# A decoder layer on one core: the loads at the start dealt to other queues, and the last column group split in two

## The chip, the cores and the metric

The kernel runs on one core of a Trainium2 chip, in one launch. The metric is the device time of the program in microseconds (us). The kernel before took 1698.23 us (median of 3 runs, 1697.18 to 1698.95). Its profiled execution took 1700.09 us, of which the span from the first to the last instruction is 1698.3 us.

The engines of a core are named as in the profile: PE is TensorE (PEld its weight loads), DVE is VectorE, ACT is ScalarE, POOL is GpSimd, SP is the engine that here issues transfers alone. A name with a q (SPq, ACTq, POOLq) is an engine's instruction queue where it issues transfers (DMA).

## What is computed

One layer of a hybrid decoder over 256 prompt tokens and 32 sample tokens (8 sequences of 4), 288 columns in all, in float32 precision:

```
proj = x @ w_in                      # D_MODEL 2048 -> 11280 columns
y_a  = (gB * conv3(gC * h)) @ w_a_out            # short convolution, with 2 rows of history
y_b  = gated_deltanet(silu(conv4(q|k|v)), ...) @ w_b_out   # 3 rows of history, state S per head
merged = sigmoid(m_a) * y_a + sigmoid(m_b) * y_b
x = layer_norm(ALPHA * x + merged @ w_o, ln1_g, ln1_b)
hid = square(relu(x @ w_up))                     # 2048 -> 8192
x = layer_norm(ALPHA * x + hid @ w_down, ln2_g, ln2_b)     # -> y_prompt, y_sample
```

The new histories and states are outputs too. The change touches how x and the histories arrive, and how the last layer norm is made.

## The kernel before

**Tiling.** Activations are held transposed: 128 features on the partitions, 16 such tiles (KT) for 2048 features, 288 columns of tokens (NT). A weight matrix is worked in groups of 256 output columns (GW). A group is cut into blocks of 4 k-tiles (KB x 128 rows x 256 columns, 512 KB). Each float32 weight is split into a high and a low part: ACT casts the block to `hi` (line 178), DVE subtracts to get `lo` (helper at line 140), and `matmuls(i)` issues three products for each k-tile and half of 128 columns: hi by x high, hi by x low, lo by x high (lines 203, 204, 205). A block is thus 8 steps of 3, 24 matmuls.

**Order.** The order is written out by hand: every engine runs its instructions in the order in which the program gives them. `blocks` lists all blocks; the loop over `i` (from line 1363) does the splits, the evacuations that are due (`at(i, f)`), then `matmuls(i)`, then the next weight load. Four buffers hold raw weights, four the high parts and four the low parts. `load(i)` is issued on SP's queue and waits until DVE has made the low part of the block that had the buffer. A list `fill` holds small jobs, and `matmuls` runs one of them after each step.

**The head.** PE turns x from rows of tokens into columns of features, in four parts `xr[0..3]` of 512 features each (`x_steps`, line 765; transposes on line 772, the high part on ACT at line 776, the low part on DVE), and the sample rows `xs4` in four pieces (`x_sample`, line 757). Part 0 is turned before the loop; parts 1 to 3 are jobs in `fill` during blocks 1, 3 and 5 (`x_fill`). The first eight blocks are interleaved so that blocks 0 and 1 need part 0, 2 and 3 part 1, 4 and 5 part 2, 6 and 7 part 3. The parts' loads stand on SP's queue between the weight loads: part 1 behind block 1's (line 737), part 2 behind block 3's (line 740), part 3 behind block 5's (line 1357). All four sample pieces are loaded from ACT's queue (lines 729 and 732). In blocks 0 to 5 the split of block i + 2 stands behind `matmuls(i)`.

The convolutions' histories and weights come by 16 loads on POOL's queue into `hwr` and `har`, each a strided piece for one quarter g of the columns, and the norm vectors by 3 more into `lnr` (lines 746 to 754). Ahead of them stands a copy of one element from `xr[2]` (line 745), so that they start when x's third part has landed. `hist_tiles` (line 792) turns them on PE ahead of block 6, lines 795, 798, 799 and, for `lnr`, 800.

**The ending.** `w_down` is worked in 4 slices of 2048 hidden features; `acc` gathers the sums over the slices together with the residual. In the last slice, `out_tiles(p)` (line 588) turns the 256 finished columns of group p back into rows of tokens, takes statistics of the prompt (line 602) and of the sample (line 618) and multiplies by the norm's gain into `Y` and `Ys`. For the sample, pieces of 128 columns from four neighbouring tiles lie as four quarters of 32 partitions; the product with the constant `quart` sums over the quarters. Group 7's evacuation and `final` (line 628) come behind the last matmul: the last 256 columns are added, turned and measured; the 16 records are aggregated (line 635); a small matrix `R` of row moments is turned (line 645) into `st5`; each of 8 output units of 128 tokens by 512 features is `Y * rs + rank1` on DVE, where `rank1` is a product of `st5` with the rows `m5` of gain and bias (line 658), and is written from SP's queue (line 696). Between the units stand the sample's steps: `moments`, `mean` (line 668), `deviation` (line 676), `scale` (lines 682 and 683) and `finish` (line 686), whose output is written by four transfers from ACT's queue (line 689).

Of the kernel before, what the change touches and what calls it, by code (L numbers as in the profile page):

```python
# [9 lines left out]
F32 = mybir.dt.float32  # L10
# [6 lines left out]
P = 128  # L17
# [23 lines left out]
def _constants():  # L41
# [31 lines left out]
    f["quart"] = (k % 32 == m % 32) * 0.25  # L73
    f["rowhi"] = np.isin(k, (0, 2, 3)) * 1.0
# [29 lines left out]
def hybrid_kernel(ctx: ExitStack, tc: tile.TileContext, A):  # L104
# [46 lines left out]
    def add_group(W, col0, row0, nk, acts, evac, width=NT):  # L151
        gi = dict(W=W, col0=col0, acts=acts, evac=evac, width=width)
        for j in range(nk // KB):
            blocks.append((gi, row0 + j * KB * P, j * KB, j == 0, j == nk // KB - 1))
# [9 lines left out]
    def load(i, step=KB):  # L164
# [4 lines left out]
        src = gi["W"][r0:r0 + KB * P, gi["col0"]:gi["col0"] + GW].rearrange("(k p) c -> p k c", p=P)  # L169
        for k in range(0, KB, step):  # L170
            sp.dma_start(t[:, k:k + step], src[:, k:k + step])
        raw[i] = t
# [14 lines left out]
    def matmuls(i):  # L187
# [7 lines left out]
        for k in range(KB):  # L195
            for t in range(2):
# [5 lines left out]
                en = last and k == KB - 1  # L202
                pe.matmul(o, wh, xh_, start=st, stop=False)  # L203
                pe.matmul(o, wh, xl_, start=False, stop=False)  # L204
                pe.matmul(o, wl, xh_, start=False, stop=en)  # L205
                if fill:
                    fill.pop(0)()
# [324 lines left out]
    def down_evac(c, p):  # L532
# [3 lines left out]
        if c == 3:  # L536
            if p == 0:
                return [f, lambda ps: None, lambda ps: out_tiles(p, ps)]
            if p == 7:
                return [lambda ps: out_tiles(p, ps)]  # L540
            hold = []

            def rest(ps):
                for g in hold:
                    for _ in g:
                        pass
                if p < 5:
                    tail_rows(p - 1)
            return [f, lambda ps: None, lambda ps: hold.extend(filter(None, [out_tiles(p, ps)])), rest]
        return [f]  # L550

    def tail_consts():
# [4 lines left out]
        gps.dma_start(ph["g2"], A["ln2_g"].to_broadcast([P, D]))  # L557
        gps.dma_start(ph["b0"], A["ln2_b"][:, 0:512].to_broadcast([P, 512]))
        gps.dma_start(ph["late"], A["cf"][:, NL:])
        for j in range(4):  # L560
            for t, n in (("gs", "ln2_g"), ("bs", "ln2_b")):
                row = A[n].rearrange("o (k j f) -> o k j f", j=4, f=P)[:, :, j, :]
                gps.dma_start(ph[t][32 * j:32 * j + 32, :].rearrange("p (k f) -> p k f", k=4),
                              row.to_broadcast([32, 4, P]))

    def tail_tiles():
        pl = ph["pool"]
        g4 = pl.tile([P, D + 256], F32R, tag="R4", name="g4")
        ph["m5"], ph["st5"] = g4[0:5, 0:D], g4[0:5, D:D + 256]
        r5 = pl.tile([P, KT * NX], F32, tag="R3", name="r5")  # L570
        ph["r5"] = r5[:, 0:2 * D].rearrange("p (a c) -> p a c", a=2)
        ph["Ys"], ph["cs"] = ph["r5"][:, 1, 0:512], ph["r5"][:, 1, 512:768]
        ph["bn"] = r5[:, 4096:4288].rearrange("p (b k s) -> p b k s", b=2, k=16)
        ph["bns"] = r5[:, 4288:4312].rearrange("p (k s) -> p k s", k=4)
        ph["sm"] = r5[:, 4320:4352]
        sp.dma_start(r5[0:3, 0:D], A["ln2_g"].to_broadcast([3, D]))
        sp.dma_start(r5[3:5, 0:D], A["ln2_b"].to_broadcast([2, D]))

    def tail_rows(n):
        c = slice(512 * n, 512 * n + 512)  # L580
        r5, m5 = ph["r5"], ph["m5"][:, c]
        raw_, lo = r5[0:5, 0, c], r5[0:5, 1, 1536:2048]
        act.copy(m5, raw_)
        tt(lo, raw_, m5, SUB)
        dve.tensor_scalar(out=m5, in0=m5, scalar1=cst("rowhi")[0:5, 0:1], scalar2=None, op0=MUL)
        stt(m5, lo, cst("rowlo")[0:5, 0:1], m5, MUL, ADD)

    def out_tiles(p, ps):
        if p == 0:
            ph["Y"] = ap_.tile([P, 2, D], F32, tag="ao", name="Y")  # L590
        Y, Ys, bn = ph["Y"], ph["Ys"], ph["bn"]
        a = ph["acc"]
        gv = [gtile()[:, 0:256].rearrange("p (b c) -> p b c", b=2) for _ in range(2)]
        if p == 7:
            for u in range(2):
                tt(a[:, 14 + u, :], a[:, 14 + u, :], ps[:, u, 0:NT], ADD)
        for u in range(2):
            for b in range(2):
                pe.transpose(gv[u][:, b, :], a[:, 2 * p + u, b * P:(b + 1) * P], ident)  # L599
        for u in range(2):  # L600
            for b in range(2):
                dve.bn_stats(out=bn[:, b, 2 * p + u, :], in_=gv[u][:, b, :])

        def scaled():
            for u in range(2):
                c = slice(256 * p + P * u, 256 * p + P * u + P)
                tt(Y[:, :, c], gv[u], bmid(ph["g2"][:, c], 2), MUL)

        w = p // 2
        if p % 2:  # L610
            cs = ph["cs"][:, (w % 2) * P:(w % 2) * P + P]
            act.copy(cs.rearrange("p (k t) -> p k t", k=4), a[:, 4 * w:4 * w + 4, NP_:NT])

        def sample():
            g2 = gtile()[:, 0:P]
            pe.transpose(g2, cs, ident)
            yield
            dve.bn_stats(out=ph["bns"][:, w, :], in_=g2)
            tt(Ys[:, w * P:(w + 1) * P], g2, ph["gs"][:, w * P:(w + 1) * P], MUL)
        if p == 7:  # L620
            ph["rest"] = scaled, sample()
            next(ph["rest"][1])
        else:
            scaled()
            if p % 2:
                return sample()

    def final():
        Y, Ys, bn, sm = ph["Y"], ph["Ys"], ph["bn"], ph["sm"]
        scaled, sample = ph["rest"]  # L630
        mv = sm[:, 0:4].rearrange("p (b s) -> p b s", b=2)
        sd, rs, r = sm[:, 4:6], sm[:, 6:8], sm[:, 8:10]
        R = ph["pool"].tile([P, 2, 5], F32R, tag="mv", name="R")
        for b in range(2):
            dve.bn_aggr(out=mv[:, b, :], in_=bn[:, b])
        act.activation(sd, mv[:, :, 1], AF.Sqrt, bias=epsc[:, 0:1])
        act.copy(R[:, :, 3:5], bc(ones[:, 0:2], 2))
        scaled()
        dve.reciprocal(out=rs, in_=sd)
        stt(r, mv[:, :, 0], -1.0, rs, MUL, MUL)  # L640
        stt(R[:, :, 0:2], bc(mv[:, :, 0], 2), -1.0, bc(rs, 2), MUL, MUL)
        tt(R[:, :, 2], r, R[:, :, 0], SUB)
        pr = gtile()
        for b in range(2):
            pe.transpose(pr[0:5, b * P:(b + 1) * P], R[:, b, :].bitcast(F32), ident)
        act.copy(ph["st5"], pr[0:5, 0:256])
# [3 lines left out]
        stt(t0, ph["g2"][:, 0:512], r[:, 0:1], ph["b0"], MUL, ADD)  # L650
        units = [(b, n) for b in range(2) for n in range(4)]
        rank1 = {0: t0}

        def prepare(i):
            if i < 8:
                b, n = units[i]
                rank1[i] = gtile()
                pe.matmul(rank1[i], ph["st5"][:, b * P:(b + 1) * P], ph["m5"][:, 512 * n:512 * n + 512],
                          start=True, stop=True)


        def moments():
            next(sample, None)
            dve.bn_aggr(out=mq, in_=ph["bns"])

        def mean():
            pq = gtile()
            pe.matmul(pq[:, 0:2], cst("quart"), mq, start=True, stop=True)
            act.copy(me, pq[:, 0:2])

        def deviation():
            tt(dv, mq[:, 0:1], me[:, 0:1], SUB)
            tt(dv, dv, dv, MUL)
            tt(vb, me[:, 1:2], epsc[:, 0:1], ADD)
            pq = gtile()
            pe.matmul(pq[:, 0:1], cst("quart"), dv, start=True, stop=True)
            act.activation(ds, pq[:, 0:1], AF.Sqrt, bias=vb)

        def scale():
            dve.reciprocal(out=qs, in_=ds)  # L680
            stt(ts, me[:, 0:1], -1.0, qs, MUL, MUL)
            act.mul(ph["gs"], ph["gs"], ts)
            gps.tensor_tensor(out=ph["gs"], in0=ph["gs"], in1=ph["bs"], op=ADD)

        def finish():
            stt(Ys, Ys, qs, ph["gs"], MUL, ADD)
            ys = A["y_sample"].rearrange("b t (k j f) -> (b t) k j f", j=4, f=P)
            for j in range(4):
                act.dma_start(ys[:, :, j, :], Ys[32 * j:32 * j + 32, :].rearrange("p (k f) -> p k f", k=4))

        steps = {0: moments, 1: mean, 2: deviation, 4: scale, 7: finish}
        prepare(1)
        for i, (b, n) in enumerate(units):
# [772 lines left out]
```

## Time and profile before

| | before |
|---|---|
| median of 3 runs | 1698.23 us |
| profiled execution | 1700.09 us |
| its span | 1698.3 us |
| mean granted PE clock | 0.994 |
| busy: PE, DVE, ACT, POOL | 99%, 60%, 43%, 8% |
| moved by DMA | 279.69 MB, mean 165 GB/s |

In a row of the timeline the columns are start and duration in us, the engine, the line of the kernel, the operation, and output <- inputs by tile name; in square brackets is the idle time of that engine just before, and what ended it. In a table of groups, `x8 | 4.7, 587 | 7.9` reads: 8 instructions, 4.7 us busy, 587 ns each, 7.9 us of idle time ahead of them. PEclk is the clock that PE was granted, 1.00 being full. A row of transfers gives the queue, how many, the size of one, and the us from issue to landing; q0 is POOL's queue of transfers, q1 SP's, q10 ACT's.

### The profile page before, as it was taken

How to read it: one execution, taken by the hardware profiler on the slowest of the kernel's cores; microseconds unless marked ns; L12 is line 12 of the kernel's file. 1: busy time of each engine (PE TensorE's matmuls, PEld its weight loads, DVE VectorE, ACT ScalarE, POOL GpSimd, SP SyncE). 2: the span in 40 equal slices, each digit the busy share in tenths (PEclk: the TensorE clock that was granted, in tenths of full speed). 3: DMA queues.
4: the chain of work that ended last, by engine and by line, in shares of the span. 5: the costliest groups of instructions: out<-in, count | busy, mean ns of one | idle time of the engine just before them, and what ended most of it. 6: DMA issues, size and time to landing. Idle time of an engine off the chain costs nothing.

```text
span 1698.3 us, 31025 instructions
## 1 busy us (share of the span) xinstructions
PE 1681.4 (99%) x13036; PEld 1665.4 (98%) x13036; DVE 1011.8 (60%) x1295; ACT 726.7 (43%) x1048; POOL 132.6 (8%) x223
## 2 busy tenths in 40 slices
PE   8999999999999999999999999999999999999997
PEld 7999999999999999999999999999999999999996
DVE  4687886757544444556778744565445554466565
ACT  4785526344533333334445533344334433344331
POOL 2231422113300000000010000000000000000000
PEclk9999999999999999999999999999999999999998
DMA  9464476535655555555575555555555555555552
GB/s 268 126 199 138 114 203 199 148 106 165 194 164 163 170 164 163 168 161 163 169 194 177 168 163 166 169 162 163 169 166 161 166 169 164 163 166 159 172 158 72
DMA packets 272997, 279.69 MB, mean 165 GB/s; under 512 B 12185, under 2 KB 268121, under 8 KB 272725
## 3 DMA queue, kind: packets, MB, share of 16 engines
q1 hardware_dynamic: 267082, 265.26, 52.4%
q0 software_dynamic: 4352, 11.67, 2.5%
q8 instruction: 102, 1.67, 0.4%
q10 hardware_dynamic: 1424, 0.79, 0.2%
q14 instruction: 37, 0.30, 0.0%
HBM read 270.19 MB, written 7.48 MB: 164 GB/s over the span
## 4 chain that ended last, share of the span: by engine, by line
PE 97%; DMA 2%; DVE 0%; issue 0%; SPq 0%; POOL 0%; ACTq 0%; ACT 0%
PE acc L203 31%; PE acc L205 31%; PE acc L204 31%; DMA xr<-in_x_prompt_dram 1%; PE g L1078 1%; DMA hwr<-in_state_gdn_conv_dram 1%; PE g L1066 0%; PE g L1225 0%; PE g L1245 0%; PE g L1248 0%; DMA lnr<-in_gdn_norm_w_dram 0%; PE g L820 0%; PE g L1197 0%; PE g L1237 0%; PE g L599 0%; PE g L947 0%
## 5 line engine op out<-in xcount | busy, mean ns | idle before, releaser
L140 DVE TENSOR_TENSOR lo<-raw,hi 128x1024 fp32r<-128x1024 f32 (+1 forms) x500 | 614.5, 1232 | 550.6 <-ACT hi L178 548.4
L178 ACT CAST hi<-raw 128x1024 fp32r<-128x1024 f32 (+1 forms) x496 | 517.2, 1045 | 760.6 <-PE acc L204 704.9
L203 PE MATMUL acc<-xh,hi 128*128 128x288 f32 x1408 | 421.9, 300 | 0.0
L204 PE MATMUL acc<-xl,hi 128*128 128x288 f32 x1408 | 416.5, 296 | 1.0 <-DVE xl L140 1.0
L205 PE MATMUL acc<-xh,lo 128*128 128x288 f32 x1408 | 416.8, 296 | 0.0
L203 PE MATMUL acc<-dh,hi 128*128 128x290 f32 x1024 | 303.9, 297 | 0.0
L204 PE MATMUL acc<-dl,hi 128*128 128x290 f32 x1024 | 303.2, 296 | 0.0
L205 PE MATMUL acc<-dh,lo 128*128 128x290 f32 x1024 | 302.7, 296 | 0.0
L205 PE MATMUL acc<-hh,lo 128*128 128x288 f32 x1024 | 302.3, 295 | 0.0
L204 PE MATMUL acc<-hl,hi 128*128 128x288 f32 x1024 | 302.3, 295 | 0.0
L203 PE MATMUL acc<-hh,hi 128*128 128x288 f32 x1024 | 302.2, 295 | 0.0
L204 PEld LDWEIGHTS acc<-xl,hi 128*128 128x128 f32 x1408 | 265.8, 189 | 2.1 <-DVE xl L140 1.2
L203 PEld LDWEIGHTS acc<-xh,hi 128*128 128x128 f32 x1408 | 265.6, 189 | 2.0 <-issue 0.7
L205 PEld LDWEIGHTS acc<-xh,lo 128*128 128x128 f32 x1408 | 265.5, 189 | 0.2 <-DVE lo L140 0.2
L203 PEld LDWEIGHTS acc<-dh,hi 128*128 128x128 f32 x1024 | 193.6, 189 | 0.1
L205 PEld LDWEIGHTS acc<-dh,lo 128*128 128x128 f32 x1024 | 193.3, 189 | 0.0
L204 PEld LDWEIGHTS acc<-dl,hi 128*128 128x128 f32 x1024 | 193.3, 189 | 0.1
L204 PEld LDWEIGHTS acc<-hl,hi 128*128 128x128 f32 x1024 | 192.5, 188 | 0.0
L205 PEld LDWEIGHTS acc<-hh,lo 128*128 128x128 f32 x1024 | 192.3, 188 | 0.0
L203 PEld LDWEIGHTS acc<-hh,hi 128*128 128x128 f32 x1024 | 192.1, 188 | 0.0
L204 PE MATMUL acc<-ml,hi 128*128 128x288 f32 x256 | 75.6, 295 | 0.0
L205 PE MATMUL acc<-mh,lo 128*128 128x288 f32 x256 | 75.6, 295 | 0.0
(395 smaller groups left out, 1606.9 us busy)
## 6 DMA issues: line engine op xcount, KB each, us to landing
raw<-in_w_in_dram SPq DMA_DIRECT2D x175, 512.0 KB, 3.8
raw<-in_w_up_dram SPq DMA_DIRECT2D x128, 512.0 KB, 3.8
raw<-in_w_down_dram SPq DMA_DIRECT2D x128, 512.0 KB, 3.7
raw<-in_w_o_dram SPq DMA_DIRECT2D x32, 512.0 KB, 4.0
raw<-in_w_a_out_dram SPq DMA_DIRECT2D x16, 512.0 KB, 3.7
raw<-in_w_b_out_dram SPq DMA_DIRECT2D x16, 512.0 KB, 3.6
S<-in_state_gdn_dram POOLq DMA_DIRECT2D x8, 512.0 KB, 6.6
out_dram<-S POOLq DMA_DIRECT2D x8, 512.0 KB, 4.6
```

The costliest lines, as they stand in the source:

```text
L140: dve.tensor_tensor(out=out, in0=a, in1=b, op=op)
L178: act.copy(his[i][:, k:k + step], raw[i][:, k:k + step])
L203: pe.matmul(o, wh, xh_, start=st, stop=False)
L204: pe.matmul(o, wh, xl_, start=False, stop=False)
L205: pe.matmul(o, wl, xh_, start=False, stop=en)
L1078: pe.matmul(out[r, q * 64:q * 64 + 64], a[r, q, :], b[r, q, :], start=True, stop=True)
```

## The change

In the head, parts 1 to 3 of x are loaded from POOL's queue, each behind a copy of one element of the part before it, so that they run in turn; three of the sample pieces follow part 1 there, and the histories follow part 3. The histories come by 4 loads of contiguous rows, with the order of rows in `hwr` and `har` changed and the copies out of PSUM rearranged to it. SP's queue holds weight loads in one row. The splits of two blocks stand together behind blocks 1, 3 and 5, behind x's copies, the even block in quarters; one empty job in `fill` is gone.

```diff
-    for c in range(1, 4):
-        act.dma_start(xs4[:, c * P:c * P + P], xsr[c])
...
-    load(1)
-    sp.dma_start(xr[1], xpr[:, :, 512:1024])
-    load(2)
-    load(3)
-    sp.dma_start(xr[2], xpr[:, :, 1024:1536])
+    for i in range(1, 4):
+        load(i)
...
-    gps.tensor_copy(hwr[0:1, 0:1], xr[2][0:1, 0, 0:1])
-    for g in range(4):
-        c, c2 = slice(768 * g, 768 * g + 768), slice(256 * g, 256 * g + 256)
-        gps.dma_start(hwr[28 * g:28 * g + 24, :], A["state_gdn_conv"][0].rearrange("b j c -> (b j) c")[:, c])
-        gps.dma_start(hwr[28 * g + 24:28 * g + 28, :], A["gdn_conv_w"][0][:, c])
-        gps.dma_start(har[19 * g:19 * g + 16, :], A["state_conv_a"][0].rearrange("b j c -> (b j) c")[:, c2])
-        gps.dma_start(har[19 * g + 16:19 * g + 19, :], A["conv_a_w"][0][:, c2])
+    for i in range(1, 4):
+        gps.tensor_copy(xr[i][0:1, 0, 0:1], xr[i - 1][0:1, 0, 0:1])
+        gps.dma_start(xr[i], xpr[:, :, 512 * i:512 * i + 512])
+        if i == 1:
+            for c in range(1, 4):
+                gps.dma_start(xs4[:, c * P:c * P + P], xsr[c])
+    gps.tensor_copy(hwr[0:1, 0:1], xr[3][0:1, 0, 0:1])
+    gps.dma_start(hwr[0:96, :], A["state_gdn_conv"][0].rearrange("b j (g c) -> (b j g) c", g=4))
+    gps.dma_start(hwr[96:112, :], A["gdn_conv_w"][0].rearrange("j (g c) -> (j g) c", g=4))
+    gps.dma_start(har[0:64, :], A["state_conv_a"][0].rearrange("b j (g c) -> (b j g) c", g=4))
+    gps.dma_start(har[64:76, :], A["conv_a_w"][0].rearrange("j (g c) -> (j g) c", g=4))
...
-    sp.dma_start(xr[3], xpr[:, :, 1536:2048])
...
-            fill.extend([idle, idle, a_, s_, idle, b_])
+            fill.extend([idle, a_, s_, idle, b_])
...
         matmuls(i)
+        if i in (1, 3, 5):
+            for u, step in ((i + 1, 1), (i + 2, KB)):
+                split_hi(u, step)
+                split_lo(u, step)
         if i < 6:
-            split_hi(i + 2)
-            split_lo(i + 2)
             load(i + 6)
```

In the ending, the last group of 256 columns becomes two groups of 128, each of 2 blocks of 8 k-tiles (the same 24 matmuls for a block). The first of them is evacuated and turned beside the last group's matmuls; its 15 records of statistics are put together early, so that `final` joins one result with one new record. Tiles 0 to 7 are no longer multiplied by the gain as rows on DVE but as columns on ACT, and are turned again in `final`, four at a time, into a PSUM tile (`widen`) onto which the product with the row moments is added (`rank`); ACT then makes the four units of them, and DVE the other four. The sample's columns are laid out with the quarter as the fastest of the row index, so that its output is one transfer.

```diff
+    def next_to_last(ps):
+        a = ph["acc"][:, 14, :]
+        tt(a, a, ps[:, 0, 0:NT], ADD)
+
+    def collect(ps):
+        turned(14)
...
+        for b in range(2):
+            dve.bn_aggr(out=fin[:, b, 1:3], in_=bn[:, b, 0:15])
...
+    def final(ps):
+        a, fin, sm, Y, Ys, R = ph["acc"], ph["fin"], ph["sm"], ph["Y"], ph["Ys"], ph["R"]
+        for c in (slice(0, P), slice(P, NP_), slice(NP_, NT)):
+            tt(a[:, 15, c], a[:, 15, c], ps[:, 0, c], ADD)
+        scaled = turned(15, fin[:, :, 3:9])
+        sample_copy(3)
+        sample_stats, sample_scaled = sample_turn(3, 4, True)
...
+        widen(0, 0)
+        widen(0, 1)
+        widen(1, 0)
+        act.activation(sd, mv[:, :, 1], AF.Sqrt, bias=epsc[:, 0:1])
...
+        def act_unit(b, n):
             c = slice(512 * n, 512 * n + 512)
-            stt(Y[:, b, c], Y[:, b, c], rs[:, b:b + 1], rank1[i], MUL, ADD)
+            act.mul(Y[:, b, c], wide[n][:, b, :], rs[:, b:b + 1])
             sp.dma_start(A["y_prompt"][0, b * P:(b + 1) * P, c], Y[:, b, c])
...
+        dve_unit(0, 2, t0)
+        rank(wide[0][:, 0], 0, 0, 0, False)
+        act_unit(0, 0)
+        pq = gtile()
+        pe.matmul(pq[:, 0:2], cst("quart"), mq, start=True, stop=True)
+        rank(wide[0][:, 1], 0, 1, 0, False)
+        act_unit(1, 0)
+        rank(wide[1][:, 0], 0, 0, 1, False)
+        act_unit(0, 1)
+        r12 = rank_tile(1, 2)
...
+        pq2 = gtile()
+        pe.matmul(pq2[:, 0:1], cst("quart"), dv, start=True, stop=True)
+        act.activation(ds, pq2[:, 0:1], AF.Sqrt, bias=vb)
+        dve_unit(1, 2, r12)
+        widen(1, 1)
+        rank(wide[1][:, 1], 0, 1, 1, False)
+        dve.reciprocal(out=qs, in_=ds)
+        stt(ts, me[:, 0:1], -1.0, qs, MUL, MUL)
+        act.mul(Ys, Ys, qs)
+        gps.tensor_tensor(out=Ys, in0=Ys, in1=ph["bs"], op=ADD)
+        act_unit(1, 1)
...
+        dve_unit(0, 3, r03)
+        dve_unit(1, 3, r13)
+        stt(Ys, ph["gs"], ts, Ys, MUL, ADD)
+        act.dma_start(A["y_sample"].rearrange("b t (j f) -> (b t j) f", j=4), Ys)
...
+    add_group(A["w_down"][0], D - 2 * P, 3 * 2048, KT, acts_h, [next_to_last, collect], cols=P)
+    add_group(A["w_down"][0], D - P, 3 * 2048, KT, acts_h, [final], cols=P)
```

The rest of the diff gives `add_group`, `load` and `matmuls` the number of columns of a group, and sets the constants and the tiles of the ending to the new layouts.

More of the change, by code (lines that the diff above doesn't have):

```diff
@@ L161, in at, with load @@
         due.setdefault(i, []).append(f)
-    def load(i, step=KB):
+    def load(i, step=16):
         if i >= len(blocks):
@@ L201, in matmuls @@
                 st = first and k == 0
[L202 removed]
+                en = last and k == kb - 1
                 pe.matmul(o, wh, xh_, start=st, stop=False)
@@ L600, in out_tiles @@
[L600 to L630, printed above, removed]
+        a, Y = ph["acc"], ph["Y"]
@@ L651, in final @@
[L651 to L669, printed above, removed]
@@ L685, in finish @@
[L685 to L693, printed above, removed]
+        for b in range(2):
+            dve.bn_aggr(out=mv[:, b, :], in_=fin[:, b])
```

211 lines of the change are left out of this document (132 added, 79 removed).

## Prediction

> **What bounds the kernel now.** I read the page first, then the waits of TensorE (PE), then the timeline where it waits.
>
> ```profile
> span 1698.3 us, 31025 instructions
> PE 1681.4 (99%) x13036; PEld 1665.4 (98%) x13036; DVE 1011.8 (60%) x1295; ACT 726.7 (43%) x1048; POOL 132.6 (8%) x223
> L203 PE MATMUL acc<-dh,hi 128*128 128x290 f32 x1024 | 303.9, 297 | 0.0
> ```
>
> PE is busy 99% of the span, and the middle's matmul groups have 0.0 us of idle time ahead of them. Asked for the waits of PE from 43 to 1680 us, the trace gives no row at all. Neither the number of product matmuls nor their shape changes, so the middle keeps its time. What can move is the first 43 us and what follows the last matmul. In the head, PE stands still at these places (start, duration, instruction, and in brackets the wait):
>
> ```profile
> 11.76 0.29 PE L205 MATMUL acc<-xh,lo 128*128 128x288 f32 x1
> 12.59 0.63 PE L772 MATMUL g<-cf,xr 128*128 128x128 f32 x4 [0.55 <-DMA xr<-in_x_prompt_dram]
> ...
> 15.74 0.40 PE L203 MATMUL acc<-xh,hi 128*128 128x288 f32 x1
> 17.15 0.40 PE L204 MATMUL acc<-xl,hi 128*128 128x288 f32 x1 [1.01 <-DVE xl L140]
> ...
> 32.22 0.26 PE L798 MATMUL g<-cf,hwr 112*128 112x112 f32 x1
> 33.41 0.26 PE L799 MATMUL g<-cf,har 76*128 76x76 f32 x1 [0.94 <-DMA har<-in_conv_a_w_dram]
> 33.61 0.23 PE L799 MATMUL g<-cf,har 76*128 76x76 f32 x1
> 35.17 0.28 PE L800 MATMUL g<-cf,lnr 33*128 33x33 f32 x1 [1.33 <-DMA lnr<-in_gdn_norm_w_dram]
> ```
>
> Two stretches behind the last of these waits (columns: stretch, its length, PE busy and instructions, then the other engines, PEclk, DMA share, GB/s):
>
> ```profile
> 35.40:41.40 6.00, 6.00 (x26) 6.00 (x26) 0.89 (x1) 0.72 (x4) 0.84 (x2) 0.50 0.89 261
> 41.60:47.60 6.00, 6.00 (x47) 6.00 (x47) 5.07 (x9) 5.43 (x11) 1.49 (x4) 1.00 0.37 109
> ```
>
> A running matmul takes 0.13 us (47 in 6.00). From start to start, less that, the waits are 0.7 + 1.3 = 2.0 us for x's second part, and 1.1 + 1.4 = 2.5 us for the histories and norm vectors. Behind these the clock falls: at a granted clock of 0.50, 26 matmuls take 6.00 us; at 1.00 they take 26 x 6.00/47 = 3.3. That is 2.7 us more. The head thus holds **2.0 + 2.5 + 2.7 = 7.2 us**. The lateness is GpSimd's (POOL): its history loads start when x's third part has landed, then wait for earlier loads of their own queue.
>
> ```profile
> 16.88 0.18 POOL L745 COPY hwr<-xr 1x1 f32<-1x1 f32 x1 [15.97 <-DMA xr<-in_x_prompt_dram]
> 17.36 0.70 POOL L748 DMA_DIRECT2D hwr<-in_state_gdn_conv_dram  x1 [0.31 <-POOL hwr L745]
> ...
> 24.25 0.52 POOL L748 DMA_DIRECT2D hwr<-in_state_gdn_conv_dram  x1 [2.66 <-DMA hwr<-in_state_gdn_conv_dram]
> ...
> 30.17 0.49 POOL L754 DMA_DIRECT2D lnr<-in_gdn_norm_w_dram  x1
> ```
>
> **The change, head.** x's parts 1 to 3 go from SP's queue to POOL's, each behind a one-element copy that waits for the part before; behind part 1 go three 64 KB loads of the sample rows (from ACT's queue), behind part 3 the histories: 4 loads instead of 16, then 3 norm loads. What 512 KB takes on either queue:
>
> ```profile
> xr<-in_x_prompt_dram SPq DMA_DIRECT2D x1, 512.0 KB, 6.2
> ```
> ```profile
> xr<-in_x_prompt_dram SPq DMA_DIRECT2D x1, 512.0 KB, 9.1
> ```
> ```profile
> S<-in_state_gdn_dram POOLq DMA_DIRECT2D x1, 512.0 KB, 5.8
> ```
> ```profile
> S<-in_state_gdn_dram POOLq DMA_DIRECT2D x2, 512.0 KB, 7.8
> ```
> ```profile
> lnr<-in_gdn_norm_w_dram POOLq DMA_DIRECT2D x1, 0.5 KB, 4.9
> ```
> ```profile
> 4.83 0.63 PE L772 MATMUL g<-cf,xr 128*128 128x128 f32 x4
> ```
>
> The first two rows are parts 1 and 2 before; the next two are a single and two queued 512 KB loads on POOL later in this kernel (KB, then us from issue to landing). I take 5.8 us a part, since only one is in flight, and keep 7.8 and SP's worst for the rivals. Part 0's first half is there by 4.8 (row L772), the copy and the step to the issue take 0.5 (16.88 to 17.36), so part 1 lands at 5.3 + 5.8 = 11.1, part 2 at 17.4, part 3 at 23.7. Seven loads follow, 0.7 us for the first issue and 0.5 for each other (rows at 17.36 and 30.17): the last starts at 27.4 and, with 4.9, lands at 32.3.
>
> When PE asks: part 1's transposes come one step (three matmuls, 0.4 us) earlier in block 1 than before, at 11.5; no wait for up to 6.2 us of landing. What comes in its place is **block 1's weights**, which sit in SP's queue when POOL's part 1 starts to move. The rows: all DMA up to 7.4 us; block 1's weights before; POOL's queue (q0) from 102 to 106 us; a weight load issued at that time.
>
> ```profile
> DMA packets 1843, 1.49 MB, mean 202 GB/s; under 512 B 128, under 2 KB 1843, under 8 KB 1843
> ```
> ```profile
> 9.46 1.14 ACT L178 CAST hi<-raw 128x512 fp32r<-128x512 f32 x2 [1.10 <-DMA raw<-in_w_in_dram]
> ```
> ```profile
> q0 software_dynamic: 317, 1.17, 101.6%
> ```
> ```profile
> raw<-in_w_in_dram SPq DMA_DIRECT2D x1, 512.0 KB, 8.0
> ```
>
> At 1.17 MB in 4 us, a part's 512 KB move in 1.8 us; half of what is left of 5.8 I put ahead of the first byte, so part 1 starts near 7.4 (an estimate). 1.49 MB had moved by 7.4 us; all up to block 1's weights is 1664 KB = 1.70 MB, so 0.2 MB are left when part 1 begins. The last two rows show such a meeting: q0 moved its 1.17 MB with no SP row beside it, and the weight load took 8.0 us. So block 1's weights, which landed at 9.46 and were just in time, may wait for part 1 (1.8 us) and the sample rows (192 KB, 0.7): between 0 and 2.5 us late. I take **1.2**, halfway, as no row shows a load that is cut off near its end. The Trainium skill, "DMA: Bandwidth & Descriptors", section "Issuing engines are not separate DMA queues", has the queues interleave on the same engines and so speaks against moving a load between them; the 102 to 106 row does not show an interleaving. By the page block 1 would be some 0.7 late instead of 1.2 (an estimate: 0.2 MB at half that row's rate take 1.4 us instead of 0.7), and the time 0.5 lower.
>
> The weight splits of blocks 2 and 3, 4 and 5, 6 and 7 now come behind x's copies on ACT and DVE, in quarters for the even block.
>
> ```profile
> L776 ACT CAST xh<-g 128x512 fp32r<-128x512 f32 x8 | 4.7, 587 | 7.9 <-PE g L772 7.9
> L140 DVE TENSOR_TENSOR xl<-g,xh 128x512 fp32r<-128x512 f32 x8 | 5.5, 689 | 11.0 <-ACT xh L776 11.0
> ...
> L140 DVE TENSOR_TENSOR lo<-raw,hi 128x256 fp32r<-128x256 f32 x4 | 1.5, 420 | 0.0
> ```
>
> From the last x transposes to the first low quarter: 0.2 + 0.59 + 0.69 + 0.42 = 1.9 us. PE has three steps (1.2) and two matmuls (0.27) to do: a wait of **0.45** at blocks 2 and 4, none at 6, where history transposes stand between. Later quarters come every 0.42 us and are used every 0.8. Parts 2 and 3 are asked for at 11.5 + 1.2 + two blocks of 24 matmuls (6.4) + x's nine transposes (about 1.0) + 0.45 = 20.5 and, by the same step without the 1.2, 28.4; they are in time. PE reaches the histories at 28.4 + 2.4 + 1.0 = 31.8, the norm vectors at 32.6, against 32.3: no wait, by 0.3 us only, and no half clock. ACT's three issues fewer gain nothing (it waits for PE there). Head: 7.2 - 1.2 - 0.9 = **5.1 us less** (bounds 3.5 and 6.7).
>
> **The change, ending.** The last 256 columns become two groups of 128, so only 128 columns' worth of sums, transposes and statistics lies behind the last matmul. Before:
>
> ```profile
> 1680.71 0.82 DVE L140 TENSOR_TENSOR acc<-acc,acc 128x288 f32<-128x288 f32 x2 [5.04 <-PE acc L205]
> ...
> 1682.50 1.02 DVE L635 BATCH_NORM_AGGREGATE r<-r 128x2 f32<-128x96 f32 x2
> ...
> 1687.42 0.59 PE L668 MATMUL g<-r,g 128*128 128x2 f32 x2
> ...
> 1689.59 0.26 ACT L677 ACTIVATE r<-g,r 128x1 f32<-128x1 f32 x1 [1.39 <-PE g L676]
> ...
> 1691.08 1.27 POOL L683 TENSOR_TENSOR g<-g 128x512 f32<-128x512 f32 x1 [822.31 <-ACT g L682]
> 1692.38 0.75 DVE L143 SCALAR_TENSOR_TENSOR r<-r,g 128x512 f32<-128x512 f32 x1
> 1693.17 2.65 ACTq L689 DMA_DIRECT2D out_dram<-r  x4
> ```
> ```profile
> L143 DVE SCALAR_TENSOR_TENSOR Y<-Y,r,g 128x512 f32<-128x512 f32 x7 | 4.9, 743 | 0.1
> ```
> ```profile
> L682 ACT ACTIVATE g<-g,r 128x512 f32<-128x512 f32 x1 | 0.7, 722 | 0.4 <-DVE r L143 0.4
> ```
>
> The prompt's eight units were 0.74 us each on DVE alone; now four stay there and four go to ACT (0.72 by L682's row; before shows no such unit from PSUM). The sample's path ends last. New, counted from 1680.7: sums 0.6, transposes and statistics to 2.0, aggregates over 9 numbers instead of 96 to 2.4 (1682.50 + 1.02 stood at 2.8), square root 2.8, row moments 3.3, their transposes and copy 4.3, sample moments 4.3, first output unit on DVE to 6.3, mean product (0.59) waiting beside it to 5.7, four small steps on DVE to 6.7, second product to 7.5, square root (0.26) 7.8, DVE's unit ahead to 8.0, two small steps 8.3, ACT 0.72 to 9.1, POOL 1.27 to 10.4, DVE 0.75 to **11.2**. Before it stood at 1693.1, 12.4: 1.2 less. Its output is one transfer of 256 KB instead of four issues in 2.65 us: one is 0.66, 2.0 less; the 2.5 us from the last issue to 1698.3 stay. The prompt's last unit ends near 10.2 and its write is covered by that. Against it: two transposes more ahead of the last matmul (four in 0.63, L772), 0.3. Ending: 1.2 + 2.0 - 0.3 = **2.9 us less** (bounds 1.2 and 4.5; the unknowns are ACT's units and the order in which PE's products interlock).
>
> **Sum.** 5.1 + 2.9 = 8.0. The profiled execution took 1700.09 for its 1698.3 us of span; that run gives 1692.1. The median shown is 1.86 below it and the terms do not depend on that: 1698.2 - 8.0 = 1690.2.
>
> **Rivals.**
> - *Block 1's weights are late and the clock halves.* The clock after the first waits:
>
> ```profile
> 16.00:20.00 4.00, 2.99 (x22) 2.85 (x22) 3.33 (x6) 2.17 (x3) 2.81 (x6) 1.00 1.09 365
> ```
>
> A wait of 2.5 instead of 1.2, in a stretch like 32.2 to 35.2, and 2.7 us of half clock: 1694.2. For: the row of q0 alone. Against: the waits up to 17.15 left the clock at 1.00. The Trainium skill, "TensorE: Matmul & The Clock Gate", Part 1, asks for an idle window of some 3.4 us; here two waits of 1.1 and 1.4 with transposes between were enough, so that rule does not exclude it. 0.12.
> - *The histories are still late.* At 6.6 us a part the norm vectors land at 34.7, PE waits 2 us, the clock falls again: head 0.4, sum 3.3, 1694.9. For: the margin of 0.3. 0.08.
> - *Slower: POOL's chain is the bound.* Three parts in series cost three times the landing: the norm vectors come at 32.3 + 3 (t - 5.8). At t = 7.7 that is 38.0, where the head loses what the ending gains; at the 7.8 of queued loads it is zero, and at 9.1, SP's slowest x part, it is 42.2, 7.2 us past before: 1702.5. Against: one part in flight, and POOL's queue went first at 102. 0.05.
> - *The ending doesn't shorten but for the one output:* sample steps wait behind units on ACT and DVE, 1691.4. 0.12, and inside the forecast's range.
> - *Block 1 isn't held up (1.2 more) and the ending reaches its bound (1.6 more):* 1687.4. 0.10.
>
> **How the numbers follow.** The forecast has 0.53, 1690.2, its own range 1688.0 to 1692.3. Eight in ten: from 1687.0 to 1694.3, which leaves out the late histories, the slow chain and half of the other edges. A measurement of this kernel can tell 0.2% (3.4 us) from no change. Faster: all but the last-named late cases, 0.90; same 0.05; slower 0.05.
>
> **What would show it.** POOL's three copies at about 5, 11 and 17 us and norm loads landing by 32; no PE wait for xr, har or lnr; one for block 1's hi or lo of 0 to 2.5 us; waits of 0.4 at blocks 2 and 4; PEclk 1.00 to the end of the head; the last DMA issued some 11 us behind the last matmul. The forecast is wrong if a part takes over 6.2 us on POOL's queue, or if the last write waits for the prompt's.

## The result and the profile after

| | before | changed |
|---|---|---|
| median of 9 runs | 1698.07 us | 1693.16 us |
| lowest and highest | 1696.32 to 1699.51 | 1692.23 to 1694.74 |
| profiled execution, its span | 1700.09, 1698.3 us | 1692.23, 1690.4 us |
| mean granted PE clock of that execution | 0.994 | 0.998 |

The ratio is 0.9973 (95% interval 0.9962 to 0.9983): 4.6 us less, between 2.9 and 6.5. The forecast, 1690.2, was 8.0 less; the measured time lies in the stated range (1687.0 to 1694.3) and above the forecast's own (1688.0 to 1692.3). From profile to profile the span fell by 7.9, nearly the forecast's sum, but the profile of before is of its longest execution and that of the changed kernel of its shortest. Where the missing 3 us are is the question of the experiments.

The page of the changed kernel:

```profile
span 1690.4 us, 31072 instructions
PE 1679.0 (99%) x13054; PEld 1663.5 (98%) x13054; DVE 1008.8 (60%) x1300; ACT 734.4 (43%) x1071; POOL 128.4 (8%) x215
```

Its waits of PE in the first 43 us (in each row the total, how often, the longest; the one for `warm` is at the very start of both kernels); then POOL's queue in the same stretch:

```profile
PE g L862 <- DMA lnr<-in_gdn_norm_w_dram: 1.2, 1, 1.2
PE g L782 <- DVE warm L777: 1.2, 1, 1.2
PE g L834 <- DMA xr<-in_x_prompt_dram: 1.0, 1, 1.0
PE acc L211 <- DVE lo L140: 0.4, 2, 0.2
```
```profile
4.95 0.88 POOL L805 DMA_DIRECT2D xr<-in_x_prompt_dram  x1 [0.31 <-POOL xr L804]
...
11.73 0.17 POOL L804 COPY xr<-xr 1x1 f32<-1x1 f32 x1 [4.25 <-DMA xr<-in_x_prompt_dram]
...
18.54 0.17 POOL L804 COPY xr<-xr 1x1 f32<-1x1 f32 x1 [5.62 <-DMA xr<-in_x_prompt_dram]
...
24.13 0.35 POOL L809 COPY hwr<-xr 1x1 f32<-1x1 f32 x1 [4.38 <-DMA xr<-in_x_prompt_dram]
24.77 0.55 POOL L810 DMA_DIRECT2D hwr<-in_state_gdn_conv_dram  x1 [0.29 <-POOL hwr L809]
...
27.86 0.49 POOL L816 DMA_DIRECT2D lnr<-in_gdn_norm_w_dram  x1
```

No wait for block 1's weights, and no wait for x's parts in the loop (the 1.0 for `xr` is for part 0, ahead of the loop). The wait for the norm vectors is still there, 1.2 us, ending at 33.66. Behind it the clock is full, where the profile of before had 26 matmuls at 0.50:

```profile
35.20:41.20 6.00, 6.00 (x47) 6.00 (x46) 4.00 (x6) 3.87 (x11) 2.67 (x5) 1.00 0.89 176
```

The ending, from the last product matmul to the last issue:

```profile
1676.26 0.29 PE L211 MATMUL acc<-hh,lo 128*128 128x288 f32 x1
```
```profile
1676.59 0.58 DVE L140 TENSOR_TENSOR acc<-acc,acc 128x128 f32<-128x128 f32 x3 [0.31 <-PE acc L211]
...
1680.85 0.75 DVE L143 SCALAR_TENSOR_TENSOR Y<-Y,r 128x512 f32<-128x512 f32 x1
...
1684.45 1.41 DVE L143 SCALAR_TENSOR_TENSOR Y<-Y,r,g 128x512 f32<-128x512 f32 x2 [0.86 <-PE g L711]
1685.77 0.75 DVE L143 SCALAR_TENSOR_TENSOR r<-g,r 128x512 f32<-128x512 f32 x1
```
```profile
1681.78 1.27 ACT L715 ACTIVATE Y<-acc,r 128x512 f32<-128x512 f32 x2 [0.58 <-PE acc L711]
...
1686.55 0.36 ACTq L758 DMA_DIRECT2D out_dram<-r  x1
```

DVE takes up the last sums at 1676.59, against 1680.71 before: 4.1 us less up to there. From there to the end of the span it is 13.8 us against 17.6: 3.8 less. ACT's new units take 0.64 to 0.69 each.

### The profile page after: what moved, and what is told of

Read it like the earlier page. It is cut to its first block, busy times and chain, and to the rows that moved or that the text cites. A ratio compares the mean times of both kernels' runs of the same rounds, so it can differ in the third digit from the quotient of the medians.

```text
span 1690.4 us, 31072 instructions
## 1 busy us (share of the span) xinstructions
PE 1679.0 (99%) x13054; PEld 1663.5 (98%) x13054; DVE 1008.8 (60%) x1300; ACT 734.4 (43%) x1071; POOL 128.4 (8%) x215
## 3 DMA queue, kind: packets, MB, share of 16 engines
q8 instruction: 102, 1.67, 0.4%
## 4 chain that ended last, share of the span: by engine, by line
PE 97%; DMA 2%; POOL 0%; issue 0%; ACT 0%; DVE 0%; DVEq 0%; SPq 0%
PE acc L209 31%; PE acc L211 31%; PE acc L210 31%; DMA xr<-in_x_prompt_dram 1%; PE g L1140 1%; PE g L1128 0%; DMA lnr<-in_gdn_norm_w_dram 0%; PE g L1287 0%; PE g L1307 0%; PE g L1310 0%; PE g L882 0%; PE g L1259 0%; PE g L1299 0%; PE g L1009 0%; PE g L615 0%
## 5 line engine op out<-in xcount | busy, mean ns | idle before, releaser
L182 ACT CAST hi<-raw 128x1024 fp32r<-128x1024 f32 (+2 forms) x505 | 517.9, 1029 | 749.7 <-PE acc L210 701.0
```

The source lines that it names most:

```text
L182: act.copy(his[i][:, k:k + step], raw[i][:, k:k + step])
```

## The experiments

All times are medians. The runs come in four sets, each on one chip, and the ratio is to runs of the kernel before in the same set. Before's median was 1697.2 in the first set (the first four rows; 30 runs), 1697.6 in the second (the next four rows; 12 runs, and one of 4222.8 us that is left out), and 1697.5 in the third (the next three) and the fourth. The theory at the start (A): the terms of the sum are right, but the half clock of before's profiled execution isn't in every run. The rival (B): the head gives its 4.1 us in every run and the ending gives less than it shows.

| kernel | median (runs) | ratio, 95% interval | clocks |
|---|---|---|---|
| head alone | 1698.00 (11) | 1.0003, 0.9994 to 1.0012 | 0.993 to 0.997 |
| ending alone | 1694.43 (11) | 0.9985, 0.9976 to 0.9994 | 0.995 to 0.998 |
| norm loads first | 1692.61 (8) | 0.9973, 0.9963 to 0.9983 | 0.997, 0.998 |
| contiguous loads alone | 1693.35 (11) | 0.9979, 0.9970 to 0.9987 | 0.996, 0.997 |
| contiguous loads and ending | 1690.27 (5) | 0.9959, 0.9946 to 0.9972 | 0.997, 0.998 |
| histories behind part 2 | 1691.53 (5) | 0.9965, 0.9952 to 0.9978 | 0.998 |
| the same, old splits | 1690.15 (5) | 0.9957, 0.9944 to 0.9970 | 0.998 |
| changed kernel again | 1693.28 (9) | 0.9975, 0.9965 to 0.9985 | 0.995 to 0.998 |
| four output transfers | 1694.43 (11) | 0.9989, 0.9980 to 0.9998 | 0.995 to 0.998 |
| old splits only | 1696.29 (11) | 0.9992, 0.9984 to 1.0001 | 0.995, 0.996 |
| before again | 1698.26 (1) | | 0.995 |
| quiet head, four transfers | 1691.31 (5) | 0.9965, 0.9952 to 0.9979 | 0.997, 0.998 |

The clock is the mean over the whole span, and the ending counts in it: behind the last product matmuls the clock halves in every profile, for 13.6 to 14.9 us with the old ending and for 5.3 to 10.0 us with the new one. The stretch is shown here for contiguous loads alone (mean clock 0.996), then for the changed kernel (0.998); both have full clock in all that stands before it.

```profile
1676.80:1691.40 14.60, 5.62 (x13) 3.00 (x13) 9.15 (x24) 1.85 (x6) 1.27 (x1) 0.50 0.47 162
```
```profile
1684.50:1690.40 5.90, 0.27 (x1) 0.00 (x0) 2.02 (x3) 0.40 (x1) 1.00 (x1) 0.50 0.74 270
```

So 0.996 with the old ending, and 0.997 or 0.998 with the new one, is what profiles show whose head has no half clock; a lower mean points to half clock in the head (0.997 can be either: the profile of norm loads first has it). Clocks are to be compared between kernels of the same ending only.

**Head alone, ending alone.** The first has every edit of the first diff, with the old ending; the second every edit of the other.

> The head of the change alone, the old ending. The profiles of before and after differ by 4.1 us up to block 7. Theory A: 2.7 us of that is the half clock behind the norm vectors' wait, and only some runs of before have it, so the median falls by 1.5 to 3 us, before's runs differ in their mean clock (0.994 and 0.996), and the slower of them are those at the lower clock. Rival B: the head gives the 4.1 us in every run, and what the medians lack (4.9 instead of 7.9) is lacking in the ending: median 4.1 lower.

> The ending alone, the old head. Profiled, the time behind the last matmul fell from 17.6 to 13.9 us, with 0.3 more for two transposes ahead of it. Theory A: the median falls by 3.2 to 3.8 us. Rival B: by some 0.8 (4.9 less 4.1). My prediction had 2.9.

The head alone gains nothing, and the ending alone 2.6 us by the ratio (1.0 to 4.1). B is out: not the ending but the head lacks its gain. But A, too, had expected 1.5 to 3 from the head.

**Norm loads first.** On the changed kernel, the three norm loads go ahead of x's parts on POOL's queue:

```diff
+    gps.dma_start(lnr[0:16, :], A["ln1_g"].rearrange("o (k p) -> (o k) p", p=P))
...
     for i in range(1, 4):
         gps.tensor_copy(xr[i][0:1, 0, 0:1], xr[i - 1][0:1, 0, 0:1])
...
-    gps.dma_start(lnr[0:16, :], A["ln1_g"].rearrange("o (k p) -> (o k) p", p=P))
...
```

> The changed kernel with the three norm loads at the front of POOL's queue instead of the end. The wait of 1.2 us for the norm vectors goes; the conv weights of har are last, issued at 24.9 and landing near 30.4, PE asks at 31.6: no wait. Theory A: 1.2 to 1.5 us less than the changed kernel's 1693.2 and no run at a clock of 0.996, since the runs at 1694.5 to 1694.7 (0.996, 0.997) had a half clock behind this wait. Rival: the lower clock of those runs comes from the ending, then some runs stay 2 us above the others, and the median is 1.2 lower.

A half miss: no run has a clock under 0.997, as expected, but the median is only 0.6 lower, not 1.2 or more, and by the ratio (0.9973, as for the changed kernel) not lower at all. The wait moved to the histories:

```profile
31.82 0.57 PE L858 MATMUL g<-cf,hwr 112*128 112x112 f32 x4 [0.66 <-DMA hwr<-in_gdn_conv_w_dram]
33.43 0.26 PE L862 MATMUL g<-cf,har 76*128 76x76 f32 x1 [0.94 <-DMA har<-in_conv_a_w_dram]
```
```profile
34.10:37.40 3.30, 3.30 (x15) 3.30 (x15) 2.20 (x2) 1.61 (x5) 1.20 (x2) 0.50 0.98 207
37.60:40.60 3.00, 3.00 (x25) 3.00 (x24) 0.68 (x1) 1.66 (x4) 0.29 (x1) 1.00 0.90 220
```

So not the norm loads are late but all that stands behind part 3. The two windows show the half clock once more (PEclk 0.50, 15 matmuls in 3.30 us against 25 in 3.00), here for some 3.4 us, about half as long as in the profile of before.

**Contiguous loads alone.** On the kernel before, only the 16 history loads become the 4 contiguous ones, with the copies out of PSUM arranged to them; x stays on SP's queue:

```diff
     gps.tensor_copy(hwr[0:1, 0:1], xr[2][0:1, 0, 0:1])
-    for g in range(4):
...
+    gps.dma_start(hwr[0:96, :], A["state_gdn_conv"][0].rearrange("b j (g c) -> (b j g) c", g=4))
...
```

> The kernel before with its 16 history loads made 4 contiguous ones, nothing else. If the number of loads made the histories late: first issue at 17.4, seven issues of 0.5 to 0.7 us end at 21, all landed by 27, PE asks at 32: the 2.5 us of waits and the half clock go, the 2.0 us of waits for x stay, so the median falls by 2.5 to 4 us, about as much as by the whole head. Rival: x has to leave SP's queue for the histories to land in time; then the norm vectors still land behind 33 and the median falls by under 1 us.

The first answer holds: 3.6 us by the ratio (2.2 to 5.1), more than the whole head and nearly as much as the whole change. POOL's queue, and PE's waits, in this kernel:

```profile
15.92 0.68 POOL L746 DMA_DIRECT2D hwr<-in_state_gdn_conv_dram  x1 [0.31 <-POOL hwr L745]
...
19.13 0.48 POOL L752 DMA_DIRECT2D lnr<-in_gdn_norm_w_dram  x1
```
```profile
PE g L719 <- DVE warm L714: 1.2, 1, 1.2
PE g L770 <- DMA xr<-in_x_prompt_dram: 0.5, 1, 0.5
PE acc L204 <- DVE xl L140: 0.4, 1, 0.4
PE acc L203 <- ACT hi L1341: 0.3, 1, 0.3
```

Seven issues end at 19.6 instead of 30.7; no wait for `hwr`, `har` or `lnr` is left. The waits for x, which I had expected to stay at 2.0 us, were 0.4 in this profile (the row for `xl`; those for `xr` and `hi` are for part 0 and block 0's weights). The edit makes the loads fewer and contiguous at once; no run here tells the two apart. For the number speaks that POOL waits for landings between the 16 loads of before (2.66 us ahead of the issue at 24.25, shown in the prediction), and never between these seven. The changed kernel has the same seven loads and starts them at 24.8, because they stand behind x's part 3 on the same queue. From this I formed theory A2: of the head only the contiguous loads gain, and moving x to POOL's queue gives it back.

**Contiguous loads and ending; histories behind part 2.** The first joins the last kernel and the new ending. The second changes one line of the changed kernel, the third also takes back the moved splits and the dropped empty job:

```diff
-    gps.tensor_copy(hwr[0:1, 0:1], xr[3][0:1, 0, 0:1])
+    gps.tensor_copy(hwr[0:1, 0:1], xr[2][0:1, 0, 0:1])
```

> The 4 contiguous loads and the new ending, with x's parts on SP's queue and the splits as before. Theory A2 (of the head only the contiguous loads gain anything; moving x to POOL's queue gives it back, since the histories then start at 24.8 instead of 15.9): the two gains add, 1693.4 (contiguous alone) less 2.8 (ending alone) = 1690.6, 6.6 under before and 2 under the changed kernel, with no run below a clock of 0.998. Rival: the moves of x and the splits are worth the 2 us of waits for x in the runs that have them: 1692.5 or more, no better than the changed kernel.

> The changed kernel with the histories waiting for x's part 2 instead of 3, so that they run beside part 3. Theory A2: issues from 19.7 to 23, landing by 30; PE asks from 30.5 to 31.6: the waits for histories and norm vectors (1.9 us in the profile of the changed kernel) go, median 1690.8 to 1691.5, no run below 0.998. Rival: part 3 and the histories share POOL's queue and part 3 lands 2 us later or more, past 28.4: the wait moves to x and the median stays at 1692.5 to 1693.

> As the kernel with the histories behind part 2, with the splits and empty jobs of before. Prices the moved splits, with the histories out of the way: if the two waits for lo of 0.2 (0.39 a block) are all that they cost, 0.8 lower than that kernel; if the old order brings back waits for x's low part at blocks 2 and 4 (0.7 and 1.0 in the profiles with the old order), 0.5 to 1 higher.

The times agree with A2 and against its rivals: 1690.27, with the clock at 0.997 or 0.998 (I had expected none below 0.998); 1691.53, all five runs within 0.5 us at 0.998; and with the old splits 1690.15. The two gains add as forecast. The cause in A2 needs one correction: the last kernel has x on POOL's queue and the first on SP's, and they are equally fast. So it isn't the move of x that gives the gain back, but the place of the histories behind x's part 3. Of the splits' price neither answer was right (1.4 us, where 0.8 was the one and a gain the other): besides the waits for lo, another wait stood behind the histories with the moved splits, seen in PE's waits and ACT's timeline of the second kernel:

```profile
PE acc L209 <- ACT w L271: 1.1, 1, 1.1
```
```profile
37.33 1.05 ACT L182 CAST hi<-raw 128x1024 fp32r<-128x1024 f32 x1 [1.67 <-DMA raw<-in_w_in_dram]
```

Paired splits free the raw buffers of two blocks late and together, so the weights behind them are loaded later, and ACT waits 1.67 us for one of those. With the old splits ACT's cast ran at 34.77 and PE did not wait there.

**The changed kernel again, and before again.**

> The changed kernel once more, for a second profile and the spread of its runs beside the others on one chip. Theory A2: most runs at 1692.3 to 1693.2 with a clock of 0.998, one in three some 2 us longer at 0.996 or 0.997, each of these with one more clock window of 3.4 us at half clock behind the norm vectors. Rival: the longer runs have the clock of the others and are longer in the ending.

> The kernel before once more, for a second profile. Theory A2: the 2.0 us of waits for x and the two windows of half clock of the first profile belong to that run; most runs of before have a clock of 0.995 or 0.996 and one window or none behind the norm vectors. This one: 1695.7 to 1698, waits for x and its low part under 1.5 us, a wait for har or lnr of 2 to 3 us as before.

The median of the changed kernel came out the same, 1693.28, and its second profile is of its longest run, 1697.78, no better than before. PE in it, and the stretch behind:

```profile
34.11 0.57 PE L857 MATMUL g<-cf,hwr 112*128 112x112 f32 x4 [2.76 <-DMA hwr<-in_gdn_conv_w_dram]
35.41 0.36 PE L861 MATMUL g<-cf,har 76*128 76x76 f32 x1 [0.63 <-DMA har<-in_conv_a_w_dram]
```
```profile
35.20:41.20 6.00, 5.72 (x24) 5.43 (x25) 1.27 (x2) 0.89 (x4) 0.25 (x2) 0.50 0.89 197
```

Part 3 had landed at 25.3 instead of 24.1, the histories followed 1.9 us later than in the first profile, PE waited 3.4 us and the clock halved. Over both sets the changed kernel has 18 runs: 11 at a clock of 0.998, 1692.18 to 1693.34 us, and 7 at 0.995 to 0.997, 1693.61 to 1697.78. So the longer runs are those with the lower clock, as expected, but the longest had two stretches of 3.4 us at half clock and not one more (the row above shows all of its 6 us at 0.50), and a wait of 0.6 for x's part 1 besides.

Before's second profile, at 0.995 and 1698.26, was 0.3 above what was expected. Its waits for x are 1.0 in the loop, against 1.6 by the same view in the first profile (0.55 and 1.01); the 0.7 for `xr` is for part 0, ahead of the loop. Its half clock was shorter: 36 matmuls in the same 6 us.

```profile
PE g L800 <- DMA lnr<-in_gdn_norm_w_dram: 2.0, 1, 2.0
...
PE acc L204 <- DVE xl L140: 1.0, 1, 1.0
PE g L772 <- DMA xr<-in_x_prompt_dram: 0.7, 1, 0.7
```
```profile
35.20:41.20 6.00, 6.00 (x36) 6.00 (x35) 0.88 (x2) 1.90 (x7) 0.55 (x2) 0.72 0.88 268
```

Of before's 30 runs in the first set, 3 had the clock of the first profile, 0.994 (1698.9 to 1699.9), 15 had that of the second, 0.995, and 12 had 0.996, which with this ending is the clock of a head without half clock; among these are the seven shortest, 1695.65 to 1696.44.

**Old splits only.** The changed kernel, histories behind part 3, with the splits of before:

```diff
-        if i in (1, 3, 5):
-            for u, step in ((i + 1, 1), (i + 2, KB)):
-                split_hi(u, step)
-                split_lo(u, step)
         if i < 6:
+            split_hi(i + 2)
+            split_lo(i + 2)
             load(i + 6)
```

> The changed kernel with the splits and empty jobs of before, histories behind part 3 as changed. With the histories behind part 2 the old splits were worth 1.4 us. Theory A2: here they are worth nothing, since the histories land at 31.5 to 33.5 whatever PE did before, and what PE gains ahead of them it waits longer there: median 1692.5 to 1693.5, and as many or more runs at 0.995 to 0.997. Rival: the two gains are independent: 1691.8.

Both answers missed: it is 3 us slower than the changed kernel, with all runs at 0.995 or 0.996. The histories did not land at a time of their own. First SP's queue and the transfers from 27 to 31 us in the changed kernel, then the same two views here:

```profile
3.77 21.40 SPq L175 DMA_DIRECT2D raw<-in_w_in_dram  x6
25.22 0.50 SPq L1409 DMA_DIRECT2D cf<-in_cf_dram  x1
```
```profile
q1 hardware_dynamic: 568, 0.80, 68.5%
q0 software_dynamic: 136, 0.42, 35.7%
```
```profile
3.75 15.18 SPq L175 DMA_DIRECT2D raw<-in_w_in_dram  x6
18.98 1.73 SPq L1409 DMA_DIRECT2D cf<-in_cf_dram  x1
```
```profile
q1 hardware_dynamic: 1044, 1.37, 98.6%
q0 software_dynamic: 16, 0.10, 7.6%
```

The landing of x's part 3 and the wait of PE in this kernel:

```profile
25.85 0.51 POOL L809 COPY hwr<-xr 1x1 f32<-1x1 f32 x1 [6.21 <-DMA xr<-in_x_prompt_dram]
```
```profile
PE g L857 <- DMA hwr<-in_gdn_conv_w_dram: 3.8, 1, 3.8
```

With the old splits the raw buffers come free earlier, SP's queue is 6 us ahead (18.98 against 25.22), and what it loads runs into x's part 3 and the histories. Part 3 lands at 25.85 instead of 24.13, though it was issued at 18.9 against 19.0, so the histories are issued 1.9 us later (26.66 against 24.77); their first bytes come 3.8 us behind that instead of 2.3, and so q0 moves 0.10 MB in those 4 us instead of 0.42. PE waits 3.8 us for `hwr`. In the changed kernel SP's queue moved next to nothing from 22.4 to 25.8: the pairing of the splits, by holding it back, kept the way clear. I take this for the reason why the same edit costs 3 us there and gains 1.4 where the histories come earlier.

**Four output transfers.** On the changed kernel, then on the kernel with the histories behind part 2 and the old splits:

```diff
-        act.dma_start(A["y_sample"].rearrange("b t (j f) -> (b t j) f", j=4), Ys)
+        ys = A["y_sample"].rearrange("b t (j f) -> (b t j) f", j=4)
+        for j in range(4):
+            act.dma_start(ys[32 * j:32 * j + 32, :], Ys[32 * j:32 * j + 32, :])
```

> The changed kernel with the sample's output in four transfers of 32 rows instead of one of 128. My prediction has the one transfer at 2.0 us less (three issues of 0.66 on ACT): 1695.2 against the changed kernel's 1693.2, and the last issue starts 2 us later behind the last matmul. Rival: smaller transfers land sooner, so less than half of the 2.0 shows: under 1694.2.

> Four output transfers once more, on the kernel with the histories behind part 2 and the old splits (1690.15, all its runs at 0.998, 0.9 us between the lowest and the highest), so that the head's clock doesn't blur it. With four transfers on the changed kernel the profile had the end 0.6 us later behind the last matmul, and its medians differed by 1.2. If the four issues (1.85 us together, against 0.36 for one) delay only the last piece, which lands sooner for its size: 1690.7 to 1691.0. Rival, my prediction's term: 1692.2.

1694.43, with clocks from 0.995 to 0.998, tells little; on the quiet head (histories behind part 2, old splits) it is 1691.31 against 1690.15, 1.2 us for the one transfer (the two were measured on different chips), between the two answers. Four issues take 1.86 us, but a transfer of 64 KB landed in 1.8 us where that of 256 KB took 2.3 (1.8 to 2.1 and 2.2 to 2.8 over the profiles):

```profile
1685.09 1.86 ACTq L760 DMA_DIRECT2D out_dram<-r  x4
```
```profile
out_dram<-r ACTq DMA_DIRECT2D x4, 64.0 KB, 1.8
```
```profile
out_dram<-r ACTq DMA_DIRECT2D x1, 256.0 KB, 2.3
```

## Why the prediction was right and where it failed

The measured time lies in the range and on the forecast side, but the forecast's sum of 8.0 became 4.6 to 4.9, and the head's part of it, 5.1, is what failed: alone it gives nothing, and on top of the new ending 1.2 us by the medians (2.0 by the ratios). That the range held is in part luck. Its upper end, 1694.3, lies just above the rival of late weights of block 1 (1694.2), which did not come; the late histories, which did, I had left out of it at 1694.9.

- *The middle keeps its time*: right; no wait of PE between 43 and 1674 us.
- *"lands at 32.3 ... no wait, by 0.3 us only, and no half clock"*: this is the step that failed. The three parts took 6.8, 6.3 and 5.1 us instead of 5.8, the last norm load was issued at 27.9 instead of 27.4 and took 5.7 us instead of 4.9, so it came at 33.6: a wait of 1.2 in the shortest run and 3.4 in the longest, with the half clock in four to seven of 18 runs by their mean clock (four at 0.996 or less, three at 0.997). The prediction's own sign of being wrong, a part of over 6.2 us on POOL's queue, came true twice in that profile. The margin was smaller than the spread of a single landing. The rival "the histories are still late" had this mechanism and got 0.08. The contiguous loads alone took the waits away.
- *"the terms do not depend on that"*: wrong. The 2.7 us of half clock were read from one execution, at 0.994; only 3 of 30 runs had that clock, 15 had the 0.995 of the second profile, with half as long a half clock, and 12 the 0.996 of none. A term that comes and goes from run to run was charged in full against the median. Within its execution the term was even too small: PEclk is 0.50 from 34.8 to 41.6 there, which costs the matmuls from 35.2 on some 3.2 us (an estimate: half of 6.4); the stretch of 6 us had cut off its ends. Shown by clock and time of each run; how much of before's median is half clock can't be read exactly from a mean rounded to 0.001.
- *Block 1's weights 1.2 late*: they were not late at all. POOL's queue moved next to nothing before 9 us, where I had put its first byte at 7.4:

```profile
q1 hardware_dynamic: 728, 0.73, 107.9%
q0 software_dynamic: 4, 0.02, 2.3%
```
```profile
q0 software_dynamic: 212, 0.68, 76.3%
q1 hardware_dynamic: 240, 0.24, 30.1%
```

The first pair is 7 to 9 us of the changed kernel, the second 9 to 11.5. So SP's queue had the way to itself until block 1 was through. The second pair also decides what I had left between the 102 to 106 row and the Trainium skill's "DMA: Bandwidth & Descriptors", section "Issuing engines are not separate DMA queues", which has the queues interleave: here both moved at once, as the page says, at three to one in bytes and about evenly in packets (the first number of each row: 212 and 240; POOL's were larger).

- *0.45 at blocks 2 and 4*: right in place, but about half the size; PE's two waits for lo are 0.2 each. That the moved splits also set when weights are loaded was not in the sum.
- *Ending 2.9*: in the profiles 3.5 (3.8 behind the last matmul, less the 0.3 for the transposes); by the ratios 2.6 alone and 3.4 on top of the contiguous loads, all within the bounds. Its parts were off against each other: the sample's path fell from 12.4 to 9.9 us, not 11.2, while the one transfer was worth 1.2 and not 2.0, since I had charged the issues and not that smaller pieces land sooner. The 9.9 depends on the clock: it is what profiles show in which the clock halves 7.8 us or more behind the start of the last sums; it is 10.3 in one where that takes 7.3 us, and 10.7 to 10.9 where it takes 6.7 or less; with the old ending it halves after 2.7 to 4.3 us. The forecast took its times for PE's small products from that half clock (0.59 for a pair, against 0.38 in the changed kernel).

Together: in the runs whose clock is that of a head without half clock (12 of before's at 0.996, 11 of the changed kernel's at 0.998), the medians are 1696.3 and 1692.6 us, 3.7 apart, about the ending's worth; what the median has beyond that, I put down to the clock. That split is an estimate, since a mean clock doesn't give the head's share of one run exactly. Open: why the head alone is no faster even in its best run (1696.06, against 1695.65 for before). Of its 11 runs 7 have a clock of 0.995 or less; that this is more than the four to seven of 18 with the new ending may be chance, or another chip.

The best versions measured are 1690.15 (histories behind part 2, old splits) and 1690.27 (before with contiguous loads and the new ending, x left where it was): 3 us below the changed kernel.

## What to carry to other kernels

When a profile shows late small loads, try first to make them fewer and contiguous where they stand; putting other loads ahead of them on their queue can use up the gain. Before a stall's aftermath (here a half clock) is put into a sum against a median, look at the mean clock of several runs: one profile may be the worst of them. And look where in the span a mean clock was lost, since here the ending alone lost more of it than the head. A margin of 0.3 us against a chain of three landings is no margin, and an edit that only moves splits also moves the weight loads behind them.

## What was not expected of the hardware

- The clock halved after short waits with work between them: 0.66 and 0.94 us (norm loads first), 2.76 and 0.63 (changed kernel again). But 0.66 and 0.77 us in the profile of four output transfers left it at 1.00, and so did one wait of 1.22 us in the changed kernel. So the length of the waits alone does not decide it; what does, no run here shows. The Trainium skill, "TensorE: Matmul & The Clock Gate", Part 1, asks for an idle window of some 3.4 us; no wait here was that long, except the 3.8 of the old splits. The half clock itself held for about 3.4 us or twice that.
- POOL's queue moves its first bytes late: 3.9 us behind the issue for x's part 1 (4.95 and 8.84) and 2.3 for the histories of the changed kernel (24.77 and 27.04), where SP's queue had moved next to nothing from 22.4 to 25.8. So the 0.10 MB of POOL's queue from 27 to 31 us with the old splits don't show that SP's queue went first: POOL's first bytes came at 30.4, and before that it may have had none to move.
- The norm load of 0.5 KB took 4.6 to 6.7 us on POOL's queue in these profiles, in front of x's parts (4.8, norm loads first) as at the end (5.7 in the changed kernel); the history load of 288 KB took 4.5 to 8.5. A small load there is not a quick one.
